# Handing the column products of a modulation vector from the planner's clock to the attention's own steps

## The chip, the cores and the metric

The kernel runs on one core of one Trainium2 chip. The metric is the device time of one execution in microseconds (us), from three runs of the same program. A profile was taken of one further execution; its times are counted from the start of its span.

## The reference, cut to what matters

One layer is computed for 640 tokens: 512 tokens of a denoising step and 128 of a context pass. The layer first makes a modulation vector, then modulates, mixes and feeds forward:

```python
mod = jax.nn.silu(cvec) @ lw['w_ada'] + lw['b_ada']
sh1, sc1, g1, sh2, sc2, g2 = jnp.split(mod, 6, axis=-1)
h = rmsnorm(x, lw['norm1_g']) * (1.0 + sc1) + sh1
mix, ... = token_mixers(h, ...)
x = x + g1 * mix
h = rmsnorm(x, lw['norm2_g']) * (1.0 + sc2) + sh2
x = x + g2 * conv_ffn(h, lw['w_up'], ...)
```

`mod` has 6 x 1024 values for each of two condition vectors, that is 48 rows of 128 values for each vector. `sh1` and `sc1` (rows 0 to 15) are needed at once; `g1`, `sh2` and `sc2` (rows 16 to 39) only after the mixers. One of the four mixers is a neighbourhood attention: each of 512 queries attends to a window of keys and to 128 context keys. The softmax is over 384 scores, computed in 16 units of 128 queries and one head.

```python
s_all = jnp.concatenate([s_win.reshape(...), s_ctx], axis=-1)
p = jax.nn.softmax(s_all, axis=-1)
out = einsum(p_win, v_win) + einsum(p_ctx, v_ctx)
```

## The kernel before, in words

**The backbone.** Large projections run on TensorE one tile of 128 output features at a time (`in_tile`, `gate_tile`; their matmuls are recorded at L362). Each tile is a chain of 48 matmuls of 128 x 320. While they are written out, `tick` moves a planner's clock `now` forward, and every side job whose due time has come is stepped once. A side job is a Python generator; what it yields is the time until it is due again. The tiles around this change are, in order, `ac`, `ax` and `ab` of the input projection, two tiles each, and then the first gate tiles.

**The column job.** `ada_cols` (L237 to L278) makes rows 16 to 39 of `mod` on VectorE (DVE). For each row f it holds 128 columns of the weight transposed in one tile of 128 x 1024, and multiplies it by the two condition vectors, which are spread over all partitions: two products per row, both recorded at L262. Product 0 writes a junk tile and product 1 writes over the weight itself. Each adds up its row into one column of `ar`. A short operation (L231, `modulate`) then turns the two sums into the row's columns of `modt`. Even rows have their weights in buffer H, odd rows from 29 on in buffer A, one buffer each. The load of row f+2 (L248, issued by SyncE's queue) is therefore written out behind product 1 of row f and waits for it. The job yields 1.4 behind each product and 2.2 behind each row, and ahead of row 35 it yields 4 more.

**The pin.** Instructions are not issued in the order in which they are written out: a list scheduler orders each engine's instructions by its own estimate of when they are ready, and prefers the one written first. `keep_in_program_order` ties an instruction behind the one that was written last on its engine. The two products carry that pin; other instructions can still pass them.

**The attention.** `attn` (L715 to L891) is a side job too. It works in pairs of units, u = 0, 2, ... 14. `s1(u)` writes out the bias sums of two units on GpSimd (L819), their score matmuls on TensorE (L827, L830), and for each unit the addition of the bias (L834), the maximum (L836) on DVE and the exponential on ScalarE (L837). `s2(u)` writes out one unit's reciprocal (L843), scaling (L844), its three transposes on TensorE (L847) and a copy out of PSUM, which is on DVE for even units (L1931) and on ScalarE for odd ones (L1929). `s3(u)` multiplies a pair's weights with the values (L864) and splits the result (L870, L871). The loop writes out s3 of the pair before, s1 of the pair after, then s2 of both units, with yields in between:

```python
        s1(0)
        yield 2 * HD[2]
        for u in range(0, 16, 2):
            if u > 0:
                s3(u - 2)
            if u < 14:
                s1(u + 2)
            ...
            yield HD[6]
            for i in range(2):
                s2(u + i)
                yield 1.2
            yield HD[8] - 0.6
```

**What waits for the column job.** The name `ada39` is set when the job ends. Three places write out all pending steps until it is there (`drain`): the last `ab` tile, `g_first`, and the first tile of the output projection.

**SyncE's queue** also carries the loads of the coming tiles' raw weights (L316, L1059). Each of these waits until one of three raw buffers is free, that is, until a DMA of GpSimd's queue (`low_dma`, recorded at L148) has read the old weight.

Of the kernel before, what the change touches and what calls it, by code (L numbers as in the profile page):

```python
# [15 lines left out]

P = 128
HY = 4
HD = [4, 5, 2.1, 7, 2.2, 1.4, 1.5, 5, 2.0, 2, 11]
NPAIR = 22  # L20
BRIDGE = 4
# [46 lines left out]
def tile_step(ctx: ExitStack, tc: tile.TileContext, a: dict, outs: list, dbg=None):  # L68
# [18 lines left out]
    jobs = []  # L87
    busy = [False]

    def pe(us):  # L90
        now[0] += us
# [17 lines left out]
    def start(gen, delay=0.0, slack=1.0):  # L109
        jobs.append([now[0] + delay, gen, slack])  # L110
# [12 lines left out]
    def nm(s):  # L123
        cnt[0] += 1
        return f"{s}_{cnt[0]}"

    def region(tag, shape, dt=F32):
        return big.tile(shape, dt, tag=tag, name=nm(tag))

    def pm():  # L130
        return psm.tile([P, 512], F32, tag="m", name=nm("m"))

    def pg():
        return psg.tile([P, 2, 512], F32, tag="g", name=nm("g"))
# [71 lines left out]
    for x in LORD.split():  # L206
# [6 lines left out]
        else:  # L213
            f = int(x)
# [11 lines left out]
    def modulate(f, x):  # L226
        if f // 8 in (0, 3):
            vec.tensor_scalar(modt[:, f, :], x, p1[:, C_BADA + f:C_BADA + f + 1], None, ALU.add)
        else:
            ng = (C_N1 if f // 8 == 1 else C_N2) + f % 8  # L230
            vec.tensor_scalar(modt[:, f, :], x, bada1[:, f:f + 1], p1[:, ng:ng + 1], ALU.add, ALU.mult)  # L231
# [2 lines left out]
    gcol = const.tile([P, 2, 2, 8], F32, name="gcol")  # L234
    growd = dram.tile([2, 16, P], F32, name="growd")

    def ada_cols(fs, tag, homes, gap, last):  # L237

        cr = region(tag, [P, 2, D])
        cf = cr.rearrange("p v c -> p (v c)")  # L240
        nc.sync.dma_start(cf, a["cc"].rearrange("v c -> (v c)").partition_broadcast(P))
        act(cf, cf, AF.Silu)
        raws = {}

        def load(f):
            if f in fs and f not in raws:
                raws[f] = homes(f)
                nc.sync.dma_start(raws[f], a["w_adt"][f - 16])  # L248

        load(fs[0])  # L250
        yield HD[4]
        for f in fs:
            load(f + 1)
            if f == 35:
                yield 4
            raw = raws.pop(f)
            ahead = f % 2 == 0 or "tots" in R or tag != "S0"
            junk = gp.tile([P, D], mybir.dt.bfloat16, tag="gt", name=nm("junk"))
            ar = sp.tile([P, 2], F32, tag="red", name=nm("ar"))
            for v in range(2):  # L260
                tc.keep_in_program_order(
                    vec.scalar_tensor_tensor(raw if v else junk, raw, 1.0, cr[:, v], ALU.mult, ALU.mult,  # L262
                                             accum_out=ar[:, v:v + 1]))
                if v and ahead:
                    load(f + 2)
                yield HD[5]
            if f // 8 in (2, 5):
                vec.tensor_scalar(gcol[:, f // 8 // 5, :, f % 8], ar, p1[:, C_BADA + f:C_BADA + f + 1],
                                  None, ALU.add)
                if f % 8 == 7:  # L270
                    yield last
                    gain_rows(f // 8 // 5)
            else:
                modulate(f, ar)
            yield gap
            while "hgrn_y" in R and "hgrn_done" not in R:
                yield 1
        R["ada%d" % fs[-1]] = True  # L278
# [9 lines left out]
    def gain_rows(i):  # L288

        m = pm()  # L290
        ten.transpose(m[0:16, 0:P], gcol[:, i].rearrange("p v f -> p (v f)"), ident)
        pe(0.11)
        g = sp.tile([16, P], F32, tag="gr", name=nm("gr"), bufs=1)
        act(g, m[0:16, 0:P], AF.Copy)
        nc.sync.dma_start(growd[i], g)
# [79 lines left out]
    def c2(ap):  # L375
        return ap.rearrange("p (c t) -> p c t", c=2)
# [4 lines left out]
    def need(tag, key, shape, dt=F32):  # L381
        if key not in R:
            R[key] = region(tag, shape, dt)
        return R[key]

    def evac_in(sec, n, ps):
# [17 lines left out]
        elif sec == "q":  # L404
            dd = need("D", "HD", [P, 2560])
            act(c2(dd[:, n * T:(n + 1) * T]), psv, AF.Silu)
# [40 lines left out]
    def hgrn():  # L447
        ff, kk, hd = R["FF"], R["KK"], R["HD"]
        he = need("E", "HE", [P, 2560])
# [25 lines left out]
        k2 = lambda d: f2(kk[:, d]).rearrange("p (n j) -> p j n", j=2)  # L475
        yield HD[9]
        for j in range(2):
# [18 lines left out]

        yield HD[0]
        tot = sp.tile([P, 2, 2, 5], F32, tag="tot", name=nm("tot"), bufs=1)
# [144 lines left out]
        R["hgrn_y"] = True  # L643
        yield HY
        for t in range(5):
# [69 lines left out]
    def attn():  # L715
# [80 lines left out]
        for h in range(4):  # L796
# [3 lines left out]
               start=True, stop=True)  # L800
# [8 lines left out]
        def s1(u):  # L809

            pr, n, _ = units_[u]
            c0 = chunk0[n]
            mg = (2, 1, 1, 0)[n]
            mv = (0, 1, 1, 2)[n]
            ms = []
            for hh_ in range(2):
                if n == 0 and pr == 1:
                    nc.sync.dma_start(eb[hh_], a["rpbe"][pr * 2 + hh_])
                pool.tensor_tensor(btt[:, hh_, 0:256], eb[hh_][:, mg * 64:mg * 64 + 256],  # L819
                                   mk[:, mv * 256:(mv + 1) * 256], ALU.add)  # L820
                ms.append(pm())
            for i in range(2):
                for hh_ in range(2):
                    b = slice(64 * hh_, 64 * hh_ + 64)
                    ql = cq[b, pr * T + n * P:pr * T + (n + 1) * P]
                    if i == 0:
                        mm(ms[hh_][:, 0:256], ql, ck[b, pr * T + c0 * 64:pr * T + c0 * 64 + 256],  # L827
                           start=True, stop=True)
                    else:
                        mm(ms[hh_][:, 256:384], ql, ckt[b, pr * P:(pr + 1) * P], start=True, stop=True)  # L830
                pe(0.32)
            for hh_ in range(2):
                s_ = sps4[(u + hh_) % 4]
                vec.tensor_tensor(s_, ms[hh_][:, 0:384], btt[:, hh_, :], ALU.add)  # L834
                st = ast[:, 12 + ((u + hh_) % 4) * 3:15 + ((u + hh_) % 4) * 3]
                vec.tensor_reduce(st[:, 0:1], s_, AX.X, ALU.max, negate=True)  # L836
                act(s_, s_, AF.Exp, bias=st[:, 0:1], accum_out=st[:, 1:2])  # L837
# [13 lines left out]
        def s3(u):  # L851

            pr, n, _ = units_[u]
            c0 = chunk0[n]
            mo = pm()
            for j in range(3):
                for hh_ in range(2):
                    h = pr * 2 + hh_
                    if j < 2:
                        i = offs.index(c0 + 2 * j)  # L860
                        v = vw[:, i * 256 + h * 64:i * 256 + h * 64 + 64]
                    else:
                        v = ccv[:, h * 64:(h + 1) * 64]
                    mm(mo[64 * hh_:64 * hh_ + 64, 0:P], v, ptt[(u + hh_) % 3][:, j * P:(j + 1) * P],  # L864
                       start=(j == 0), stop=(j == 2))
                    pe(0.15)
            hv = yc[:, 0, pr, 0:TS].rearrange("p (r n c) -> p n r c", r=8, n=4)[:, n]
            lv = yc[:, 1, pr, 0:TS].rearrange("p (r n c) -> p n r c", r=8, n=4)[:, n]
            mov = mo[:, 0:P].rearrange("p (r c) -> p r c", r=8)
            act(hv, mov, AF.Copy)  # L870
            vec.tensor_tensor(lv, mov, hv.bitcast(F32), ALU.subtract)  # L871

        s1(0)
        yield 2 * HD[2]
        for u in range(0, 16, 2):
# [4 lines that stand above are left out]
                s1(u + 2)  # L880
            else:
                R["scores"] = True
            yield HD[6]
            for i in range(2):
                s2(u + i)
                yield 1.2
            yield HD[8] - 0.6
        s3(14)
        nc.sync.dma_start(o_ck[0, 0].rearrange("h s d -> s h d"), ktk.rearrange("p (h d) -> p h d", h=4))
        nc.sync.dma_start(ycd, yc.bitcast(F32))  # L890
# [11 lines left out]
    def in_tile(sec, n, w):  # L902
        ps = pg()
        gemm(ps, w, 0, 8, xhk, xlk)
        evac_in(sec, n, ps)
        if n == 1:
            R[sec + "_done"] = True
        if n == 1 and sec in starts:
            start(starts[sec](), 1.5, SLACK[sec])
            if sec == "cv":  # L910
                start(g_operands())
            if sec == "q":
                start(ada_cols(range(16, 40), "S0", col_home, HD[4], 10), HD[7])

    def tok_tile(sec, kh, w):

# [1195 lines left out]
    for i in range(3):  # L2112
        sec, n = SECTIONS[i // 2], i % 2
# [107 lines left out]
```

## Time and profile before

| what | value |
| --- | --- |
| three runs | 1024.14, 1024.87 and 3496.3 us; median 1024.87 us |
| the profiled execution | 1023.97 us |
| its span | 1022.1 us, so 1.87 us lie around it |
| mean granted TensorE clock | 0.998 of full speed |
| DVE busy over the span | 790.1 us (77%) |
| ScalarE busy over the span | 538.6 us (53%) |
| GpSimd busy over the span | 106.5 us (10%) |

The profile names engines PE (TensorE's matmuls), PEld (its weight loads), DVE, ACT, POOL and SPq (SyncE's queue). A matmul's end is modelled, so a busy PE is not a PE at its peak; a wait of PE shows as idle time ahead of an instruction, with the instruction that ended it. The attention's units run from 222 to 287 us of the span. Rows 35 to 39 of the column job, ten products, run between 228 and 267 us; rows 16 to 34 run before the attention's first scores.

### The profile page before, as it was taken

What the parts mean: (1) busy time and instruction counts of PE and PEld (TensorE: products, weight loads), DVE (VectorE), ACT (ScalarE), POOL (GpSimd) and SP (SyncE); (2) the same over time, 40 slices, a digit from 0 to 9 for tenths busy, and PEclk for the clock granted to TensorE, in tenths of its full rate; (3) what the DMA queues carried; (4) which work ended last, traced back from release to release, by engine and by line L of the source; (5) the groups of instructions that cost most, each with busy time, mean ns of one, the idle gap of its engine ahead of it and who ended that gap; (6) DMA issues with size and microseconds to landing.
All of it is one profiled execution on the core that took longest, in us unless ns stands there. A gap on an engine that the chain in (4) does not pass through costs nothing.

```text
span 1022.1 us, 18764 instructions
## 1 busy us (share of the span) xinstructions
PE 1008.3 (99%) x7572; PEld 951.9 (93%) x7572; DVE 790.1 (77%) x1308; ACT 538.6 (53%) x933; POOL 106.5 (10%) x153
## 2 busy tenths in 40 slices
PE   8999999999999999999999999999999999999997
PEld 6899999999899999999998899999999999888886
DVE  6758899769866676767868879998888887796644
ACT  6642343354555444444544567777777776634432
POOL 1000020312100000000010111111112221001101
PEclk9999999999999999999999999999999999999999
DMA  9864433597562413323179584765555669974212
GB/s 354 322 221 127 126 124 114 171 263 216 143 206 79 155 52 104 130 77 104 49 282 349 207 328 112 195 163 150 150 151 149 154 161 271 370 259 146 83 42 103
DMA packets 55926, 177.85 MB, mean 174 GB/s; under 512 B 8192, under 2 KB 14624, under 8 KB 53280
## 3 DMA queue, kind: packets, MB, share of 16 engines
q1 hardware_dynamic: 45008, 140.60, 39.6%
q0 software_dynamic: 10832, 36.06, 14.8%
q8 instruction: 59, 0.97, 0.4%
q14 instruction: 27, 0.22, 0.1%
HBM read 134.93 MB, written 25.46 MB: 157 GB/s over the span
## 4 chain that ended last, share of the span: by engine, by line
PE 91%; DVE 5%; DMA 1%; issue 1%; ACT 1%; POOL 1%; SPq 0%; POOLq 0%; DVEq 0%; ACTq 0%
PE g L1478 19%; PE m L1122 17%; PE g L362 14%; PE g L1813 8%; PE m L1813 6%; PE g L1135 5%; PE m L1478 4%; PE m L1262 3%; PE g L933 2%; PE g L1262 2%; PE m L148 2%; PE g L148 1%; PE m L1473 1%; PE m L526 1%; DMA A<-in_w_ada_dram 1%
## 5 line engine op out<-in xcount | busy, mean ns | idle before, releaser
L362 PE MATMUL g<-XH,w 128*128 128x320 f32 x704 | 171.4, 317 | 0.0
L362 PEld LDWEIGHTS g<-XH,w 128*128 128x128 f32 x704 | 120.6, 188 | 2.4 <-issue 1.2
L362 PE MATMUL g<-XL,w 128*128 128x320 f32 x352 | 108.8, 309 | 0.0
L362 PEld LDWEIGHTS g<-XL,w 128*128 128x128 f32 x352 | 66.3, 188 | 0.0
L311 DVE TENSOR_TENSOR w<-raw,w 128x1024 fp32r<-128x1024 f32 x34 | 41.4, 1221 | 14.9 <-ACT w L310 9.1
L1122 PE MATMUL m<-XH,w 128*128 128x320 f32 x224 | 52.5, 309 | 0.0
L1813 PE MATMUL g<-w,XH 128*128 128x512 f32 (+1 forms) x216 | 50.2, 385 | 0.0
L1813 PEld LDWEIGHTS g<-w,XH 128*128 128x128 f32 x216 | 39.5, 188 | 8.3 <-ACT XH L1772 0.3
L310 ACT ACTIVATE w<-raw 128x1024 fp32r<-128x1024 f32 x34 | 35.7, 1050 | 21.3 <-PE g L1262 10.0
L1813 PE MATMUL g<-w,XL 128*128 128x512 f32 (+1 forms) x180 | 42.4, 386 | 0.0
L148 DVE SCALAR_TENSOR_TENSOR X<-MG,p2t,X 128x641 f32<-128x641 f32 x44 | 38.9, 885 | 4.3 <-ACT X L148 3.4
L148 DVE SCALAR_TENSOR_TENSOR X<-X,p2t,X 128x641 f32<-128x641 f32 x44 | 38.9, 884 | 1.9 <-ACT X L148 1.0
L1813 PEld LDWEIGHTS g<-w,XL 128*128 128x128 f32 x180 | 33.4, 188 | 7.1 <-DVE dt L1828 0.2
L148 ACT ACTIVATE w<-raw 128x1024 fp32r<-128x1024 f32 (+3 forms) x46 | 38.2, 851 | 2.7 <-DMA raw<-in_w_in_dram 1.7
L1478 PE MATMUL g<-XL,w 128*128 128x320 f32 x240 | 38.6, 310 | 0.0
L1478 PE MATMUL g<-XL,C 128*128 128x320 f32 x240 | 38.4, 309 | 0.0
L1122 PEld LDWEIGHTS m<-XH,w 128*128 128x128 f32 x224 | 38.3, 188 | 0.0
L1478 PEld LDWEIGHTS g<-XL,w 128*128 128x128 f32 x240 | 36.0, 188 | 0.5 <-ACT MG L148 0.3
L1813 PE MATMUL m<-w,XH 128*128 128x512 f32 (+1 forms) x156 | 36.4, 381 | 0.0
L1478 PEld LDWEIGHTS g<-XL,C 128*128 128x128 f32 x240 | 35.9, 188 | 0.4 <-ACT MG L148 0.4
L1122 PE MATMUL m<-XL,w 128*128 128x320 f32 x112 | 34.6, 309 | 0.0
L1813 PEld LDWEIGHTS m<-w,XH 128*128 128x128 f32 x156 | 28.5, 188 | 5.6
(549 smaller groups left out, 2751.9 us busy)
## 6 DMA issues: line engine op xcount, KB each, us to landing
raw<-in_w_up_dram SPq DMA_DIRECT2D x30, 512.0 KB, 4.9
raw<-in_w_gp_dram SPq DMA_DIRECT2D x21, 640.0 KB, 4.0
raw<-in_w_down_dram SPq DMA_DIRECT2D x22, 512.0 KB, 4.0
raw<-in_w_in_dram SPq DMA_DIRECT2D x19, 512.0 KB, 4.2
H<-in_w_adt_dram SPq DMA_DIRECT2D x16, 512.0 KB, 4.5
actd<-X POOLq DMA_DIRECT2D x22, 320.5 KB, 5.4
X<-in_w_adt_dram SPq DMA_DIRECT2D x10, 512.0 KB, 4.0
upd<-XL SPq DMA_DIRECT2D x4, 1280.0 KB, 6.4
```

What stands on the lines that cost most here:

```text
L148: r = f(*args, **kw)
L310: act(w[0], raw, AF.Copy)
L311: vec.tensor_tensor(w[1], raw, w[0].bitcast(F32), ALU.subtract)
L362: mm(o, w[:, h, k0 + k, :], r(k)[:, s], start=(k == 0 and i == 0), stop=(k == kt - 1 and i == 2))
L526: mm(m[W * g:W * g + W, (i - s0) * W:(i - s0 + 1) * W], lhs, rhs, start=True, stop=True, tile_position=(64 * par, W * g))
L933: mm(o, x(kx)[:, ts], w[:, h, k, :], start=(kx == 0 and i == 0), stop=(kx == 7 and i == 2))
L1122: mm(o, w[:, k, :], x[:, k, :], start=(first and k == 0 and j == 0), stop=(k == 3 and j == 2), skip_group_check=True)
L1135: mm(pb[:, c, 0:HC], w[:, h + k, :], y[:, x, k, s], start=(k == 0 and j == 0), stop=(k == 1 and j == 2))
L1262: mm(m, mh[k // 2][:, hx, k % 2, t * P:(t + 1) * P], wo[q][:, hw, k % 2, :], start=(k == 0 and i == 0), stop=(k == 7 and i == 2))
L1473: mm(o, w[:, k, :], x[:, k, :], start=(first and not part and k == 0 and j == 0), stop=(part == 1 and k == 3), skip_group_check=True)
L1478: z = mm(o, w[:, k, :], x[:, k, :], start=(first and k == 0 and j == 0), stop=(k == 3 and j == 2), skip_group_check=True)
L1813: mm(ps, sl[k][hx][:, t * P:(t + 1) * P], w[:, hw, k, c0:c1], start=first, stop=end and (last or nh == 1 and t == 4 and kk_ == 7))
```

## The change

The attention's loop takes the column job out of the planner's list when it reaches its first scores, and steps it itself from then on. `col_step` runs the generator on until one product has been written out. It is called at two places of each pair: once directly behind `s1`, which ends with the maxima of two units, and once behind the two `s2`. What is left after the last pair would be run out in a row. The yields inside the column job no longer count there, and the extra pause ahead of row 35 is gone. No instruction is added or removed.

```diff
+COLS = (16, 16)
...
+    cols, colj = [0], []
+
+    def col_step():
+        n = cols[0]
+        while colj and cols[0] == n:
+            try:
+                next(colj[0])
+            except StopIteration:
+                colj.clear()
+
     def ada_cols(fs, tag, homes, gap, last):
...
         for f in fs:
             load(f + 1)
-            if f == 35:
-                yield 4
             raw = raws.pop(f)
...
                     vec.scalar_tensor_tensor(raw if v else junk, raw, 1.0, cr[:, v], ALU.mult, ALU.mult,
                                              accum_out=ar[:, v:v + 1]))
+                cols[0] += 1
                 if v and ahead:
                     load(f + 2)
                 yield HD[5]
...
+        mine = [j for j in jobs if colj and j[1] is colj[0]]
+        for j in mine:
+            jobs.remove(j)
+        if not mine:
+            colj.clear()
         s1(0)
         yield 2 * HD[2]
         for u in range(0, 16, 2):
...
                 s1(u + 2)
             else:
                 R["scores"] = True
+            if u < COLS[0]:
+                col_step()
             yield HD[6]
             for i in range(2):
                 s2(u + i)
                 yield 1.2
+            if u < COLS[1]:
+                col_step()
             yield HD[8] - 0.6
+        while colj:
+            col_step()
+            yield 1.4
         s3(14)
...
             if sec == "q":
-                start(ada_cols(range(16, 40), "S0", col_home, HD[4], 10), HD[7])
+                colj.append(ada_cols(range(16, 40), "S0", col_home, HD[4], 10))
+                start(colj[0], HD[7])
```

## The prediction

> **What bounds the kernel now.** I read the page first.
>
> ```profile
> span 1022.1 us, 18764 instructions
> PE 1008.3 (99%) x7572; PEld 951.9 (93%) x7572; DVE 790.1 (77%) x1308; ACT 538.6 (53%) x933; POOL 106.5 (10%) x153
> ```
>
> TensorE has something to do for 1008.3 of 1022.1 us. The change adds and removes no instruction, so it can gain only what TensorE waits for, and it can lose whatever it makes TensorE wait for. So I took the busy times by stage around the attention, and then the waits of TensorE there (205 to 300 us).
>
> ```profile
> 200.00:220.00 20.00, 19.44 (x142) 18.95 (x142) 14.26 (x32) 10.12 (x19) 3.16 (x4) 1.00 0.90 265
> 220.00:240.00 20.00, 20.00 (x155) 18.55 (x154) 14.31 (x34) 9.96 (x23) 6.04 (x8) 1.00 0.94 274
> 240.00:260.00 20.00, 19.75 (x150) 17.57 (x148) 19.96 (x50) 9.09 (x17) 5.03 (x7) 1.00 0.80 220
> 260.00:280.00 20.00, 19.72 (x163) 17.56 (x163) 16.85 (x39) 9.58 (x21) 4.48 (x6) 1.00 0.47 110
> ```
>
> ```profile
> PE m L847 <- DVE X L844: 0.4, 2, 0.2
> PEld m L847 <- DVE X L844: 1.0, 2, 0.5
> ```
>
> The columns of the stages are the length, then busy time and count of PE, PEld, DVE, ACT and POOL, the granted clock, the DMA share and GB/s. PE is busy for 19.72 us or more in each of the three stages that hold the attention, at a clock of 1.00. The first wait row is all that the matmuls wait for: the transposes (L847) wait 0.4 us in total for a scaling (L844) on DVE. The second row, 1.0 us, is the same two waits seen by the weight loads, which partly run beside matmuls. Between 240 and 260 us DVE is full: 19.96 of 20 us. There an order on DVE can cost TensorE time, and nowhere else in the attention is it that close.
>
> **Where the ten products stand now.** The next three fences are DVE in order of time, for row 35, row 37, and row 38 with the first product of row 39.
>
> ```profile
> 227.98 1.00 DVE L836 TENSOR_REDUCE ast<-X 128x1 f32<-128x384 f32 x2
> 228.90 1.29 DVE L262 SCALAR_TENSOR_TENSOR junk<-A,S 128x1024 bf16<-128x1024 f32 x1
> 230.12 0.55 DVE L1931 COPY B<-m 128x384 f32<-128x384 f32 x1
> 230.59 1.21 DVE L262 SCALAR_TENSOR_TENSOR A<-A,S 128x1024 f32<-128x1024 f32 x1
> 231.87 0.27 DVE L231 TENSOR_SCALAR modt<-ar,bada,cst 128x2 f32<-128x2 f32 x1
> ```
>
> ```profile
> 243.99 0.99 DVE L836 TENSOR_REDUCE ast<-X 128x1 f32<-128x384 f32 x2
> 244.91 1.57 DVE L262 SCALAR_TENSOR_TENSOR junk<-A,S 128x1024 bf16<-128x1024 f32 x1
> 246.41 0.55 DVE L1931 COPY B<-m 128x384 f32<-128x384 f32 x1
> 246.87 1.21 DVE L262 SCALAR_TENSOR_TENSOR A<-A,S 128x1024 f32<-128x1024 f32 x1
> ```
>
> ```profile
> 252.79 1.21 DVE L262 SCALAR_TENSOR_TENSOR junk<-H,S 128x1024 bf16<-128x1024 f32 x1
> 253.94 0.41 DVE L844 TENSOR_SCALAR X<-X,ast 128x384 f32<-128x384 f32 x1
> ...
> 255.19 0.55 DVE L1931 COPY B<-m 128x384 f32<-128x384 f32 x1
> ...
> 256.58 1.22 DVE L262 SCALAR_TENSOR_TENSOR H<-H,S 128x1024 f32<-128x1024 f32 x1
> ...
> 258.04 0.74 DVE L844 TENSOR_SCALAR X<-X,ast 128x384 f32<-128x384 f32 x2
> ...
> 263.95 1.22 DVE L262 SCALAR_TENSOR_TENSOR junk<-A,S 128x1024 bf16<-128x1024 f32 x1
> ```
>
> Product 0 of a row already stands right behind a pair's maxima (L836, then L262 at 228.90 and at 244.91). Product 1 already stands right behind the DVE copy of the pair's transposes (L1931, then L262 at 230.59 and 246.87). That is what the change prescribes. The planner's clock has met the pattern by itself, one row per pair; the pause ahead of row 35 is what set the phase. So the change writes down a place that the products mostly have.
>
> **The change part by part.**
>
> *The pause.* The attention takes the job over at its first scores, and the yields stop counting there. Row 35's product 0 is then written out behind the next pair's maxima, where it stands at 228.90. Cost 0; the cover is that no place moves.
>
> *Product 0 of rows 35 to 39.* It stays the last thing written out in front of s2(u). Cost 0 on both sides.
>
> *Product 1.* It moves from between the two s2 to behind both, and its pin moves from the copy L1931 to the scaling of the odd unit, L844. For rows 35 and 37 that scaling is long done when product 0 runs, so product 1 may now stand on either side of the copy; the scheduler prefers the copy, which is written first, and I expect the order of now. Bound on the bad side: the copy comes 1.21 us later (the 246.87 row). The tightest pair then delays the product with the values, L864, which begins here:
>
> ```profile
> 248.12 0.66 PE L864 MATMUL m<-B,X 128*64 128x128 f32 x8
> 254.40 0.55 PE L847 MATMUL m<-cst,X 128*128 128x128 f32 x3 [0.25 <-DVE X L844]
> 258.60 0.52 PE L847 MATMUL m<-cst,X 128*128 128x128 f32 x3
> ```
>
> The copy ends at 246.41 + 0.55 = 246.96, and 248.12 - 246.96 = 1.16 us lie behind it. A copy later by 1.21 us costs 0.05 us there. The worst that five such flips can do, if no pair had any cover, is 5 x 1.21 = 6.1 us; the nearest row says about 0.1, and I take 0.
>
> In row 38's pair something does move. Product 1 (256.58) now stands ahead of scalings at 258.04, one of them the odd unit's, which lets its transposes begin at 258.60. Written behind that scaling, product 1 gives it 1.22 us back. TensorE had other matmuls in between, so the bounds are 0 and the whole wait of the two rows of L847, 0.4 us. The wait at 254.40 hangs on product 0 and stays. I take -0.2.
>
> *The short operation L231.* It is now written out with the next product 0, a pair later: five of 0.27 us. No step of this stage reads it, and it comes ahead of its old place only where DVE is free: cost 0. Uncovered, in the full stage, it would be 2 x 0.27 = 0.5 us.
>
> *The loads.* The load of row f+2 is written out behind both s2 instead of between them, and waits for product 1. This is SyncE's queue, in order of time, and below it the landings of the loads at 231.84, 241.45 and 251.31 us, each from its own issue:
>
> ```profile
> 231.84 0.33 SPq L248 DMA_DIRECT2D A<-in_w_adt_dram  x1
> 240.08 0.33 SPq L316 DMA_DIRECT2D raw<-in_w_gate_dram  x1
> ...
> 241.45 0.38 SPq L248 DMA_DIRECT2D H<-in_w_adt_dram  x1
> 250.89 0.33 SPq L316 DMA_DIRECT2D raw<-in_w_gate_dram  x1
> 251.31 0.38 SPq L248 DMA_DIRECT2D A<-in_w_adt_dram  x1
> ```
>
> ```profile
> DMA to landing us min/median/max: 7.9/7.9/7.9
> DMA to landing us min/median/max: 9.6/9.6/9.6
> DMA to landing us min/median/max: 7.9/7.9/7.9
> ```
>
> Row 37 lands at 231.84 + 7.9 = 239.7 and is wanted at 244.91: 5.2 us to spare. Row 38 lands at 241.45 + 9.6 = 251.05 and is wanted at 252.79: 1.7 us. Row 39 lands at 251.31 + 7.9 = 259.2 and is wanted at 263.95: 4.7 us. A product 1 that is later by a scaling of 0.41 to a product of 1.2 us stays inside all of these: cost 0, with row 38 the closest. DVE takes its instructions in order, so a product whose row is late holds up the scalings behind it, and TensorE's transposes behind those.
>
> [...] Row 37's product 0 took 1.57 us where the others take about 1.22, while GpSimd ran a bias sum:
>
> ```profile
> 244.66 0.72 POOL L819 TENSOR_TENSOR B<-X 128x256 f32<-128x256 f32 x1 [2.96 <-DVE ast L836]
> ```
>
> [...]
>
> *The sum.* 0 + 0 + 0 - 0.2 + 0 + 0 = -0.2 us, against the profiled execution's own 1023.97 us (its span of 1022.1 and 1.87 around it): 1023.8 us. The shown runs of 1024.14 and 1024.87 us lie 0.2 and 0.9 above that execution, so a median of some runs should stand about 0.4 above the sum: **1024.2 us**. A measurement of this kernel tells about 2%, some 20 us, from no change; this is far inside.
>
> **The rivals.**
>
> *A load slips behind the next raw load (slower).* Row 38's load goes in right behind the raw load at 240.08. The next raw load, at 250.89, is the one whose wait fills the queue behind it:
>
> ```profile
> SPq L316 <- DMA w<-raw: 31.0, 4, 9.0
> ```
>
> These are waits of up to 9.0 us each (228 to 262 us). If the scheduler now puts row 38's load behind that raw load, it is issued at 251.3 and lands 7.9 to 9.6 us later, at 259.2 to 260.9. Product 0 then holds DVE from 252.79 on for 6.4 to 8.1 us; the scaling at 253.94 and the transposes at 254.40 stand behind it, and TensorE's order is fixed, so all of it shows: 1030.6 to 1032.3, say 1031.4 us. For it: the load is now written out later, near the tile boundary where the raw load is. Against it: the raw load of 250.89 was ready late even so, and product 1 moves by 1.2 us at most in a gap of 9. It decides from the point at which product 1 of row 36 is ranked behind that raw load. [...]
>
> *The waits go (faster).* The steadier order takes all of L847's waits, matmuls and weight loads: 0.4 + 1.0 = 1.4 us, and 1023.97 + 0.4 - 1.4 = 1023.0 us in the measure of the forecast. For it: both products cease to separate the units of row 38's pair. Against it: the larger wait, 0.25 of 0.4, hangs on product 0, which stays.
>
> *The copies flip (slower by little).* Product 1 goes ahead of the copy in all pairs, and half of the 1.21 us finds no cover in two of them: +1.2, and 1025.6 us. Against it: the copy is written first.
>
> *It doesn't do what it says.* The phase is off by a pair, row 35 running in front of the first scores once its pause is gone. Then all rows end a pair earlier, and only row 35's own landing matters; against it the order in the code, in which the job yields 2.2 behind row 34 and the first scores are written out in that time. Time as the forecast, 1024.2 us within 1.
>
> **How the numbers follow.** The forecast as it stands (1023.3 to 1025.2 us) has 0.63, the faster rival 0.13, the flip 0.11, the phase 0.04, the slipped load 0.07, and 0.02 are left for what I do not see. The range takes in the first four and the measurement's own spread of about 0.7 us between the two close runs, widened for a scheduler whose other choices may shift: 1021.8 to 1027.8 us. The slipped load stays outside. Over 2% faster would need over 20 us, which TensorE does not wait: 0.01, for the unseen alone. Over 2% slower needs three slipped loads: 0.02. Within 2%: 0.97.
>
> **What would show it.** Right: ten products behind the attention's first scores, product 0 right behind L836 in five pairs; product 1 of row 38 behind both scalings; the three loads still each ahead of the next raw load; L847's matmul waits at 0.4 us or less; span within 1.5 us of 1022.1. Wrong: idle DVE that a load of the weights ends; a PE wait above 1 us between 222 and 290 us; a copy L1931 behind product 1; or a span that moves while this stage does not.

## The result

| | before | after |
|---|---|---|
| median of the runs | 1024.53 us over four runs, of which one took 3496.3; the other three 1024.14 to 1024.87, median 1024.2 | 1035.75 us (1035.30 to 1036.22) |
| the profiled execution's own time | 1023.97 us | 1035.8 us |
| its span | 1022.1 us | 1034.0 us |
| mean granted clock | 0.998 | 0.994 |

The ratio is 1.0111, with a 95% interval of 1.0091 to 1.0131. The change costs 11.2 us by the medians, 11.6 us against the three close runs. This is within 2%, as expected, but 8.0 us above the upper end of the range, 1027.8 us, and so outside it. The forecast of 1024.2 us is wrong.

The page after, its totals and its row of granted clocks:

```profile
span 1034.0 us, 18763 instructions
PE 1013.2 (98%) x7572; PEld 956.7 (93%) x7572; DVE 790.1 (76%) x1308; ACT 539.3 (52%) x933; POOL 106.1 (10%) x153
...
PEclk9999999998999999999999999999999999999999
```

The busy time of DVE is the same to the tenth, 790.1 us, so no work came in. PE is busy for 4.9 us more than before, and its clock has a dip in the tenth slice, 233 to 258 us. The busy times by stage, in the columns of the prediction's table, show where:

```profile
220.00:240.00 20.00, 20.00 (x156) 18.55 (x154) 15.43 (x38) 9.97 (x23) 6.06 (x8) 1.00 0.96 272
240.00:260.00 20.00, 14.85 (x106) 13.55 (x106) 14.71 (x35) 6.30 (x14) 4.59 (x6) 0.83 0.80 211
260.00:280.00 20.00, 19.79 (x154) 17.55 (x154) 15.73 (x38) 9.34 (x18) 3.76 (x5) 1.00 0.33 86
280.00:300.00 20.00, 16.93 (x122) 15.77 (x119) 13.46 (x22) 10.92 (x17) 1.76 (x2) 0.91 0.33 79
```

Before, the last of these stages read:

```profile
280.00:300.00 20.00, 20.00 (x147) 19.45 (x144) 15.50 (x18) 11.31 (x14) 0.87 (x1) 1.00 0.64 197
```

Two stages are hurt. Between 240 and 260 us PE is idle for 5.15 us and its clock falls to 0.83. Between 280 and 300 us, behind the stages that the prediction showed, it is idle for 3.07 us at a clock of 0.91. The waits of TensorE from 205 to 320 us name what ended each (total, times, longest):

```profile
PE m L858 <- DVE X L855: 5.4, 2, 5.1
...
PE g L373 <- ACT gt L995: 3.1, 1, 3.1
```

L858 and L855 are the transposes and the scaling that were L847 and L844. Before, they waited 0.4 us; L373, the matmul of the gate's projection, did not wait at all.

**The first wait.** DVE in order of time. L232 is the short operation, L272 the products:

```profile
231.89 0.27 DVE L232 TENSOR_SCALAR modt<-ar,bada,cst 128x2 f32<-128x2 f32 x1
232.07 1.21 DVE L272 SCALAR_TENSOR_TENSOR junk<-H,S 128x1024 bf16<-128x1024 f32 x1
...
239.60 0.27 DVE L232 TENSOR_SCALAR modt<-ar,bada,cst 128x2 f32<-128x2 f32 x1
239.86 1.23 DVE L272 SCALAR_TENSOR_TENSOR junk<-A,S 128x1024 bf16<-128x1024 f32 x1
...
245.41 0.28 DVE L232 TENSOR_SCALAR modt<-ar,bada,cst 128x2 f32<-128x2 f32 x1
250.98 1.23 DVE L272 SCALAR_TENSOR_TENSOR junk<-H,S 128x1024 bf16<-128x1024 f32 x1 [5.29 <-DMA H<-in_w_adt_dram]
...
255.09 0.42 DVE L855 TENSOR_SCALAR X<-X,ast 128x384 f32<-128x384 f32 x1
```

Product 0 of rows 36 to 39 now stands right behind a short operation and no longer behind a pair's maxima; row 35's is still behind its maxima, at 228.92 us. Row 37's runs at 239.86 instead of 244.91. Row 38's is next on DVE at 245.69 (245.41 + 0.28), 7.1 us ahead of its old place at 252.79, and holds DVE for 5.29 us until its weights are there. The scaling at 255.09 is queued behind it, with some 3 us of the convolution's work in between. The load itself is not late. SyncE's queue after:

```profile
241.65 0.38 SPq L260 DMA_DIRECT2D H<-in_w_adt_dram  x1
243.00 0.33 SPq L260 DMA_DIRECT2D A<-in_w_adt_dram  x1
250.37 0.33 SPq L327 DMA_DIRECT2D raw<-in_w_gate_dram  x1
```

Row 38's load goes out at 241.65, before at 241.45, and still ahead of the next raw load. The product came early; the load did not slip.

TensorE's rows show the wait, then matmul pairs of 0.73 us that take 0.45 at full clock, and then the second wait:

```profile
255.66 0.87 PE L858 MATMUL m<-cst,X 128*128 128x128 f32 x3 [5.15 <-DVE X L855]
...
256.86 0.73 PE L373 MATMUL g<-XH,w 128*128 128x320 f32 x2
...
260.36 0.45 PE L373 MATMUL g<-XH,w 128*128 128x320 f32 x2
...
293.52 0.42 PE L373 MATMUL g<-XH,w 128*128 128x320 f32 x1 [3.07 <-ACT gt L995]
```

**The second wait.** ScalarE ahead of 293.52, after and then before (L149 was L148, L995 was L971):

```profile
290.95 0.42 ACT L149 ACTIVATE H<-raw 128x256 fp32r<-128x256 f32 x1 [3.66 <-DMA raw<-in_w_gp_dram]
291.38 1.28 ACT L995 ACT_TABLE_LOAD   x1
292.68 0.80 ACT L995 ACTIVATE gt<-g,cst 128x640 f32<-128x640 f32 x1
```

```profile
281.95 0.80 ACT L971 ACTIVATE gt<-g,cst 128x640 f32<-128x640 f32 x1
...
289.81 0.40 ACT L148 ACTIVATE H<-raw 128x256 fp32r<-128x256 f32 x1
```

The sigmoid of the first gate tile (L995) and a copy of branch weights (L149) have changed places in ScalarE's order. The copy waits for its DMA, and the sigmoid, for which PE waits, stands behind it.

**The sum.** The two waits give 5.4 + 3.1 - 0.4 = 8.1 us. Behind each follows a stretch at half clock, as these windows show:

```profile
255.60:259.80 4.20, 4.14 (x17) 4.18 (x18) 4.20 (x11) 1.31 (x4) 1.41 (x2) 0.51 0.50 115
...
293.50:296.90 3.40, 3.38 (x14) 3.38 (x15) 2.68 (x4) 3.40 (x4) 0.00 (x0) 0.56 0.00 0
```

The lost part of the clock is 0.49 x 4.2 = 2.1 us and 0.44 x 3.4 = 1.5 us. Together 11.7 us, against 11.9 us in the spans. That leaves 0.2 us.

### The profile page after: what moved, and what is told of

Read it like the earlier page. It is cut to its first block, busy times and chain, and to the rows that moved or that the text cites. A ratio compares the mean times of both kernels' runs of the same rounds, so it can differ in the third digit from the quotient of the medians.

```text
span 1034.0 us, 18763 instructions
## 1 busy us (share of the span) xinstructions
PE 1013.2 (98%) x7572; PEld 956.7 (93%) x7572; DVE 790.1 (76%) x1308; ACT 539.3 (52%) x933; POOL 106.1 (10%) x153
## 4 chain that ended last, share of the span: by engine, by line
PE 90%; DVE 4%; DMA 3%; issue 1%; ACT 1%; POOL 1%; SPq 0%; POOLq 0%; DVEq 0%; ACTq 0%
PE g L1502 19%; PE m L1146 17%; PE g L373 14%; PE g L1837 8%; PE m L1837 6%; PE g L1159 5%; PE m L1502 4%; PE m L1286 3%; PE g L957 2%; PE g L1286 2%; PE m L149 2%; PE g L149 1%; PE m L1497 1%; PE m L537 1%; DMA A<-in_w_ada_dram 1%
## 5 line engine op out<-in xcount | busy, mean ns | idle before, releaser
L373 PE MATMUL g<-XH,w 128*128 128x320 f32 x704 | 175.2, 322 | 3.1 <-ACT gt L995 3.1
L373 PEld LDWEIGHTS g<-XH,w 128*128 128x128 f32 x704 | 123.2, 192 | 5.8 <-ACT gt L995 3.3
L373 PE MATMUL g<-XL,w 128*128 128x320 f32 x352 | 110.1, 313 | 0.0
L373 PEld LDWEIGHTS g<-XL,w 128*128 128x128 f32 x352 | 67.6, 192 | 0.0
L149 DVE SCALAR_TENSOR_TENSOR X<-MG,p2t,X 128x641 f32<-128x641 f32 x44 | 38.9, 884 | 4.3 <-ACT X L149 3.4
L149 DVE SCALAR_TENSOR_TENSOR X<-X,p2t,X 128x641 f32<-128x641 f32 x44 | 38.9, 884 | 1.9 <-ACT X L149 1.0
L149 ACT ACTIVATE w<-raw 128x1024 fp32r<-128x1024 f32 (+3 forms) x46 | 38.5, 852 | 2.1 <-DMA raw<-in_w_in_dram 1.1
```

The lines of the kernel that those rows point to most:

```text
L149: r = f(*args, **kw)
L373: mm(o, w[:, h, k0 + k, :], r(k)[:, s], start=(k == 0 and i == 0), stop=(k == kt - 1 and i == 2))
```

## The experiments

The theory from the trace: in the changed kernel a row's first step begins with the short operation of the row before, and only then writes out product 0, so the pin ties product 0 to the short operation, which is ready early, instead of to the maxima. The rivals: that the early place does no harm and the load was at fault, that the missing pause shifted everything, and that the second wait is a consequence of the first.

In the list, "the stage" is the time from the attention's first score matmul to the end of the span. It leaves out what lies ahead of all changed instructions. Before it is 1022.1 - 222.34 = 799.8 us, after it is 1034.0 - 222.35 = 811.7 us.

**e1: the short operation goes back behind product 1.** A kernel after in which the second step runs on through the short operation, so that a row's first step writes out product 0 alone:

```diff
-                cols[0] += 1
+                cols[0] += 1 - v
...
                 modulate(f, ar)
+            cols[0] += 1
             yield gap
```

> The changed kernel, with one difference: the second step of a pair runs on until the short operation L231 of that row is written out too, so that the next row's product 0 finds the pair's maxima as the last thing written on DVE. Theory (the pin is taken by the short operation): product 0 of rows 36 to 38 returns behind the maxima, no product waits for a load, TensorE's wait of 5.1 us and the one of 3.1 us are gone, clock 1.00 throughout, 1023.5 to 1025.0 us. Rival (the handover itself, or loads that are written out later, make row 38's load late): the wait for row 38's load stays, 1033 us or more.

1029.72 us (1027.24 to 1030.07, 5 runs), ratio to before 1.0044 (1.0030 to 1.0059). TensorE's waits:

```profile
PE g L374 <- ACT gt L996: 3.2, 1, 3.2
PE m L859 <- DVE X L856: 0.5, 1, 0.5
```

The 5.1 us wait is gone, no product waits for a load, and row 38's product 0 is behind its maxima again. So far the theory holds. Its time was missed, because the second wait stayed at full size: the copy still stands ahead of the sigmoid. The second wait is not a consequence of the first. The stage of the profiled run, 1028.3 - 224.00 = 804.3 us, is 4.5 us longer than before; the rest of that run's excess lies ahead of the first score (see e9).

**e3: the kernel before with the short operation written late.** The pause, the planner and the places of the products stay; only the short operations of rows 35 to 38 are written directly ahead of the next product 0:

```diff
-            else:
+            elif f not in range(35, 39):
                 modulate(f, ar)
             yield gap
+            if f in range(35, 39):
+                modulate(f, ar)
```

> The kernel before, job in the planner's list and pause as they were, with one difference: L231 of rows 35 to 38 is written out directly ahead of the next row's product 0 instead of 2.2 of the planner's clock earlier. Theory: this alone frees product 0 from the maxima; products of rows 36 to 38 run up to a pair early, row 38's waits for its load by 2 to 5 us, and the time is 1028 to 1036 us. Rival (the handover or the missing pause does it): 1024 to 1025 us.

1027.68 us (one run), span 1025.9 us, the stage 3.6 us longer than before. One row of DVE, and one of TensorE:

```profile
251.15 1.23 DVE L262 SCALAR_TENSOR_TENSOR junk<-H,S 128x1024 bf16<-128x1024 f32 x1 [1.29 <-DMA H<-in_w_adt_dram]
```

```profile
255.50 0.52 PE L849 MATMUL m<-cst,X 128*128 128x128 f32 x3 [2.31 <-DVE X L846]
```

The same fault appears in the kernel before by moving one operation of 0.27 us: row 38's product 0 goes early, waits for its load, and the transposes wait 2.31 us. So neither the handover nor the missing pause is needed for the first wait, and the load, issued at 241.54 us, was not late. The size was 0.3 us below the lower edge of what the theory gave: here the short operation of row 37 ran at 249.58 instead of 245.41, so the product was only 1.29 us early for its load.

**e4: the kernel after without row 38's load.** Row 38 reads what row 36 left in the buffer, so its columns come from other weights:

```diff
         def load(f):
-            if f in fs and f not in raws:
+            if f == 38:
+                raws.setdefault(f, raw)
+            elif f in fs and f not in raws:
```

> The changed kernel without the load of row 38: its products read what is left in row 36's buffer, so the columns of row 38 are not the reference's. DVE's order stays that of the changed kernel. Theory (the cost is the wait for that load, and what follows from it): no DVE wait at row 38, no TensorE wait of 5.1 us, clock 1.00 there; 1024 to 1025 us if the later wait of 3.1 us follows from it, 1028 to 1030 us if that one has a cause of its own. Rival (products a pair early cost by their place on a full DVE): 1032 us or more.

1030.79 us (one run), span 1028.9 us, 0.8 us above the 1028 to 1030 of a second wait with its own cause; the first score of this run came at 223.70 us, 1.4 us later than before (see e9).

```profile
PE g L375 <- ACT gt L997: 3.0, 1, 3.0
PE m L860 <- DVE X L857: 0.6, 2, 0.4
```

With the products left early and only the load gone, the first wait is gone. The second stays with its half clock (0.91 between 280 and 300 us).

**e5: the kernel after with one tie on ScalarE.** The first branch copy is tied in program order, so that it cannot pass the sigmoid:

```diff
-            oact(b[:, 0:2], x[:, 8:10], AF.Copy)
+            z = oact(b[:, 0:2], x[:, 8:10], AF.Copy)
+            if p_ == 0:
+                tc.keep_in_program_order(z)
```

> The changed kernel, with one difference: the first copy of the gate stage's branch weights (ScalarE, H<-raw) is tied behind what is written out ahead of it on ScalarE. In the changed kernel it stands ahead of the first gate's sigmoid and waits 3.7 us for its weights. Theory (the second wait is a matter of ScalarE's order, its own cause beside the first): TensorE's wait of 3.1 us goes with its 3.4 us at half clock, the wait of 5.1 us stays: 1030 to 1032 us. Rival (the second wait only passes on the delay of the first through SyncE's queue): a wait of about 3 us appears at another place of that stage, 1034 to 1036 us.

1030.91 us (one run), span 1028.8 us. One wait and two windows:

```profile
PE m L858 <- DVE X L855: 5.0, 2, 4.8
```

```profile
240.00:260.00 20.00, 15.17 (x107) 13.86 (x106) 14.98 (x35) 6.33 (x14) 4.79 (x6) 0.83 0.86 231
280.00:300.00 20.00, 20.00 (x155) 19.10 (x152) 16.46 (x24) 12.85 (x18) 1.76 (x2) 1.00 0.51 148
```

As expected: the second wait and its half clock go, the first stays. The two causes are separate, each with its own mend.

**e7: both mends.** The edits of e1 and e5 together.

> The changed kernel with both mends: the short operation written out with product 1, and the first branch copy tied on ScalarE. Theory (two causes, and no third): no TensorE wait above 0.6 us from 205 to 320 us, clock 1.00 there, 1023.5 to 1025.0 us, the same as before within 0.1%. Rival (the handover costs something of its own): 1026 us or more with these two waits gone.

1023.32 us (1022.96 to 1023.98, 11 runs) against 1024.29 us for the kernel before in the same comparison; ratio 0.9989 (0.9980 to 0.9998). All that TensorE waits for, and the two stages:

```profile
PE m L859 <- DVE X L856: 0.5, 1, 0.5
```

```profile
240.00:260.00 20.00, 19.46 (x154) 17.25 (x152) 20.00 (x48) 8.95 (x17) 4.67 (x6) 1.00 0.76 198
280.00:300.00 20.00, 20.00 (x144) 19.62 (x144) 14.66 (x18) 11.32 (x14) 0.87 (x1) 1.00 0.65 203
```

The two causes are all of the loss. The median is 0.2 us under the lower edge of what was expected. It is the lowest of all the kernels, ahead of the one before by 0.1%, an amount that the interval only just sets apart from nothing.

**e8: e7 with product 0 between the two s2.** The first step moves from behind the maxima to behind the even unit's s2, so that its scaling no longer stands behind a product:

```diff
-            if u < COLS[0]:
-                col_step()
...
                 s2(u + i)
+                if i == 0 and u < COLS[0]:
+                    col_step()
```

> As the kernel with both mends, but the first step of a pair is written out behind the even unit's scaling instead of behind the maxima, so that product 0 stands behind the copy L1931 and the even unit's scaling goes ahead of it. Theory: the wait of the transposes for a scaling (0.3 to 0.5 us) goes too: 0.3 to 0.6 us under the kernel with both mends, at the edge of what can be measured. Rival (that wait comes from the convolution's work on the full DVE): the same time as that kernel within 0.2 us.

1023.57 us (1022.80 to 1025.63, 11 runs), ratio 0.9994 (0.9985 to 1.0003). The 0.5 us wait does go, and PE waits for nothing between 205 and 320 us. Span 1021.3 against 1021.8 us for e7; the medians do not tell the two apart, so the gain of 0.3 to 0.6 us did not show.

**e9: no load of row 38, and the tie on ScalarE.** The edits of e4 and e5. The products are as early as in the kernel after, and nothing waits for the load. Again row 38's columns come from other weights.

> The changed kernel without the load of row 38 (its products read row 36's buffer, so row 38's columns are not the reference's) and with the branch copy tied on ScalarE; the products stay a pair early. Theory (an early place costs only by its wait for a load): 1023.5 to 1025.2 us. Rival (an early product 0 pushes scalings back on a full DVE): 1026 us or more, with TensorE waits for scalings of over 1 us in sum.

1025.91 us (one run), span 1023.8 us, 0.7 us above what the theory gave. The transposes hardly wait:

```profile
PE m L860 <- DVE X L857: 0.2, 1, 0.2
```

But the first score, ahead of anything that was changed, came later in this execution than before:

```profile
224.01 0.70 PE L840 MATMUL m<-F 64*128 64x256 f32 x4
```

```profile
222.34 0.70 PE L827 MATMUL m<-F 64*128 64x256 f32 x4
```

The stage takes 1023.8 - 224.01 = 799.8 us, as long as before. So in this run early products cost nothing; it is the early product whose load has not landed that does. The same late start (224.00 and 223.70 us) lies in the profiles of e1 and e4. In e9 TensorE waits 0.8 us for the load of `cst` and 0.9 us for that of `C`, for which it does not wait in the profiles of before, after, e6, e7 and e8. Why it waits there was not studied.

**e6: the kernel before without its pause.** No handover, only

```diff
             load(f + 1)
-            if f == 35:
-                yield 4
             raw = raws.pop(f)
```

> The kernel before without the pause ahead of row 35, and nothing else. Theory (the pause set only the phase; its removal has no part in the loss): rows 35 to 39 run about half a pair earlier, each behind a pair's maxima, since the short operation is written out well ahead of them; row 36, whose load landed at 232.0 us before, may wait 1 us on DVE; 1024 to 1026 us. Rival (the pause protected row 35 or 36 from its load): a DVE wait of 3 us or more ended by a row's load, 1027 us or more.

1030.45 us (one run), span 1028.6 us, the stage 6.5 us longer. This expectation fell. TensorE's waits, DVE's products, and a window:

```profile
PE g L360 <- ACT gt L969: 3.3, 1, 3.3
...
PE m L845 <- DVE X L842: 2.1, 2, 1.9
```

```profile
232.02 1.23 DVE L260 SCALAR_TENSOR_TENSOR junk<-H,S 128x1024 bf16<-128x1024 f32 x1 [0.57 <-DMA H<-in_w_adt_dram]
...
239.22 1.22 DVE L260 SCALAR_TENSOR_TENSOR junk<-A,S 128x1024 bf16<-128x1024 f32 x1 [1.16 <-DMA A<-in_w_adt_dram]
...
254.83 1.21 DVE L260 SCALAR_TENSOR_TENSOR junk<-A,S 128x1024 bf16<-128x1024 f32 x1
```

Without the pause every row runs early: row 36 at 232.02 (237.12 before), row 37 at 239.22 (244.91), row 39 at 254.83 (263.95). Row 39's products now fall into the stage in which DVE was full already. Nine products instead of seven stand ahead of the scaling for which TensorE waits 1.9 us; it runs at 255.97 us instead of 253.94. That the two products make this wait is read from the order, and no run shows it alone. The wait of over 3 us for a load, by which the rival would have worked, did not come: the longest is the 1.16 us above. The copy passes the sigmoid here too. So the pause by itself was not idle: it held the rows in their places. In e1, with the pause gone as well, the handover holds them instead.

**e10: e1 with product 1 between the two s2.** The pause is gone and the attention has the job, but product 1 is written where it was written before, and there is no tie on ScalarE:

```diff
                 yield 1.2
-            if u < COLS[1]:
-                col_step()
+                if i == 0 and u < COLS[1]:
+                    col_step()
```

> The changed kernel with the short operation written out with product 1, and product 1 written out between the two s2 as before; the branch copy on ScalarE is not tied. There is no pause here, and the attention steps the job. Theory (the ScalarE order is a close race in the scheduler's estimate, which the place of product 1 tips): the first gate's sigmoid is back ahead of the branch copy, no TensorE wait of 3 us, clock 1.00, 1023.5 to 1025.0 us. Rival (the missing pause or the handover tips it): the wait of about 3 us and 3.4 us at half clock, 1028.5 to 1030 us.

1024.25 us (1023.93 to 1025.12, 11 runs), ratio 1.0003 (0.9994 to 1.0012). TensorE's only wait:

```profile
PE m L859 <- DVE X L856: 0.2, 1, 0.2
```

The sigmoid stands ahead of the copy (281.95 and 289.80 us), as before. So the handover and the missing pause cost nothing by themselves. What tips ScalarE's order from e10 to e1 is the written place of the second step alone: product 1, with the next load and the short operation written out behind it.

**e11: the kernel before with a pause of 3 instead of 4.**

```diff
             if f == 35:
-                yield 4
+                yield 3
```

> The kernel before with a pause of 3 in place of 4 ahead of row 35, and nothing else. Theory (the planner's own pattern held only by its phase): products 0 of rows 36 and 38 lose their place behind the maxima as in the changed kernel, TensorE waits for scalings by 1 us or more, and the branch copy may come ahead of the sigmoid: 1026 to 1034 us. Rival (the pause as such costs nothing, as forecast): 1024 to 1025 us.

1034.14 us (one run), span 1032.3 us, 0.1 us above what the theory gave.

```profile
DVE junk L262 <- DMA H<-in_w_adt_dram: 7.5, 1, 7.5
```

```profile
PE m L864 <- DVE B L1931: 6.6, 1, 6.6
PE g L362 <- ACT gt L971: 3.1, 1, 3.1
```

One unit of the planner's clock less, and both faults are there again, with nothing else changed: row 38's product 0 waits 7.45 us for its weights, and the copy passes the sigmoid. The first comes about in another way than in the kernel after: this product 0 stands right behind scalings (241.58 us) and ahead of row 37's product 1 (252.97 us), not behind a short operation. What the two kernels share is the early product whose load has not landed. The kernel before stood on a narrow ledge.

## Why the prediction was wrong

**The step that failed** is "*Product 0 of rows 35 to 39.* It stays the last thing written out in front of s2(u). Cost 0 on both sides." It is the last thing written out, but not the only thing: the short operation is written out between the maxima and product 0, and takes the pin. The companion step says it of "*The short operation L231*": "It is now written out with the next product 0, a pair later … cost 0". I priced its 0.27 us and the readers of its result, and did not ask who is tied behind it. Measured: 5.0 us of waiting more (5.4 in place of 0.4) and 2.1 us of half clock. e1 takes it away, e3 puts it into the kernel before.

**The scope failed as well.** I searched for waits in the attention and took the rest of the program as fixed ("widened for a scheduler whose other choices may shift" was the only allowance, up to 1027.8). The second loss, 3.1 + 1.5 us, is such a choice, on ScalarE, some 30 us behind row 39's first product. e5 takes it away. Either loss alone goes beyond the range: about 7 and 5 us, over the 3.6 that the range left above the forecast.

**The rival of the slipped load** had the right kind of wait and the wrong place. It foresaw a product 0 of row 38 that holds DVE for 6.4 to 8.1 us, with the transposes behind it: measured 5.29 us. But it wanted the load late at 251.3, and it was issued at 241.65. The distance between product and load shrank from the product's side: row 38's 1.7 us to spare, worked out in the prediction, became a lack of 5.3 us when the product came 7.1 us sooner. That row 38 was the closest of the three was right.

**The rival of the phase** had the rows a pair early, much as products 0 of rows 36 to 38 came to run (5.0 to 7.1 us sooner), and priced that at nothing because "only row 35's own landing matters". Row 38's landing mattered, by 5.29 us.

**The pause**: cost 0 was right beside the handover (e10), and row 35's product 0 kept its place. Without the handover the pause does matter (e6, e11).

**Product 1**: the written place behind both s2 was put at -0.2 us and at most 6.1. In row 38's pair it went behind both scalings as I said, at 260.91 after the scaling at 258.74, but the kernel after hides any gain. In e7, which has it there, the odd unit's scaling begins at 257.30 us, against 258.03 in e10, which has not; TensorE did not wait at that place in either, so nothing is gained. The 0.5 us that e7 waits lies at the even unit's scaling, behind product 0. The real cost of the new place came on another engine, by the order on ScalarE (e1 against e10).

**A longer product 0**, like row 37's of 1.57 us before, had no part in the loss: row 38's took 1.23 us in the kernel after. Back behind its maxima it took 1.31 to 1.32 us (e1, e7, e10), so 0.1 us more.

**The faster rival** added 0.4 and 1.0 us, which are the same two waits seen twice; the sum had 0.4 us to win at most.

**The signs** named for a wrong forecast are those that came: idle DVE that a load of the weights ends, and a PE wait above 1 us. "The three loads still each ahead of the next raw load" came true and helped nothing.

**The half clock** had no term in the sum: before, the granted clock was 1.00 in all four stages. Measured are 2.1 and 1.5 us behind the two waits (0.51 over 4.2 us and 0.56 over 3.4 us).

Why the scheduler's estimate puts the copy ahead of the sigmoid in e1 and after, and behind it before and in e10, stays open. That it is a close choice is shown by e11 and e6, which tip it from a part of the program far off; the estimate itself was not looked into.

## What to carry to other kernels

A pin "behind the last instruction written" is only as good as that instruction: when a step is moved, list everything that it writes out, in order, and look for what now stands between the pin and the place it should mark, above all an operation that is ready early. A product that may start early must have its load landed by then, or it holds up its engine, as row 38's product 0 did DVE for 5.29 us in the kernel after and for 7.45 us in e11. And where a list scheduler orders the engines, a change of written place can tip a close choice on another engine far behind it: tie those choices that the time depends on, as e5 does, before judging the change itself.

## What the runs showed of the hardware

In several runs TensorE's granted clock fell near a wait: in the kernel after it is 0.50 from 252.9 to 259.7 us. With that 0.50, the time at half clock is estimated as 2 x 20 us x (1 - granted clock) of the windows:

| kernel | TensorE waits | granted clock | at half clock (estimate) |
|---|---|---|---|
| after | 5.15 us | 0.83 in 240 to 260 us | 6.8 us |
| e5 | 4.8 us | 0.83 in 240 to 260 us | 6.8 us |
| after | 3.07 us | 0.91 in 280 to 300 us | 3.6 us |
| e1 | 3.2 us | 0.91 in 280 to 300 us | 3.6 us |
| e4 | 3.0 us | 0.91 in 280 to 300 us | 3.6 us |
| e3 | 2.31 us | 0.91 in 240 to 260 us | 3.6 us |
| e6 | 1.9 us | 0.94 in 240 to 260, 0.97 in 260 to 280 us | 3.6 us |
| e6 | 3.3 us | 1.00 in 280 to 300 us | none |
| e11 | 6.6 us | 0.83 in 240 to 260 us | 6.8 us |
| e11 | 3.1 us | 1.00 in 280 to 300 us | none |

Near a wait of 1.9 us (e6) lie about 3.6 us at half clock, near those of 3.1 us (e11) and 3.3 us (e6) none. Length alone does not decide. Nor does the stretch begin where the wait ends: in the kernel after the clock is 0.50 from 252.9 to 259.7 us, while the wait ends at 255.66, so that 2.1 of the 3.4 us lost fall on matmuls. The five runs of e1, one kernel, have mean clocks of 0.994 to 0.998, so the same waits may cost more or less clock from run to run; only one of the five was profiled. The rows of e3 and of e6's last stage:

```profile
240.00:260.00 20.00, 17.68 (x128) 16.38 (x127) 18.49 (x43) 6.48 (x14) 5.60 (x6) 0.91 0.80 216
```

```profile
280.00:300.00 20.00, 16.74 (x126) 15.74 (x125) 13.68 (x21) 11.18 (x16) 0.87 (x1) 1.00 0.39 115
```

What decides beside the length was not shown.

Product 0 of row 37 did not take the same time in every run. Before, a GpSimd sum of 0.72 us began at 244.66 us, and the product that began at 244.91 on DVE took 1.57 us. In e10 the product began at 245.12 and took 1.21 us; there GpSimd was busy for 6.24 us between 240 and 260 us, with seven instructions, against 5.03 us with seven before. Whether the two engines stretched each other was not shown.
